# Five tap buffers instead of four, two gated tiles instead of three, and the decay sums one to a weight block

## The chip, the cores and the metric

The kernel runs on one core of one Trainium2 chip. The metric is the device time of one execution in microseconds (us), from the first instruction to the last with what lies around them. Five engines work at once, each through its own queue of instructions in order: PE (TensorE, matmuls; PEld is its weight load), DVE (VectorE), ACT (ScalarE), POOL (GpSimd) and SP (which issues DMAs).

## The reference, cut to what matters

One encoder block over 16 + 1024 tokens of width 1024. The part that the change touches is the start of the mixer: one wide projection, and then a depthwise convolution of 31 taps over the gated values (the conformer branch), a depthwise convolution of 7 taps (the state-space branch), and decays of a chunked state-space scan in both directions.

```python
u = h @ w_in
g_val, g_gate, z, xs, bs, cs, dtf, dtb, gate_conv, gate_ssm = jnp.split(u, offs, axis=-1)
a = g_val * jax.nn.sigmoid(g_gate)
a = dwconv(a, conv_dw_w, conv_dw_b)                      # 31 taps
a = jax.nn.silu(layernorm(a, conv_ln_g, conv_ln_b))
y_conv = a @ conv_out_w
xbc = jax.nn.silu(dwconv(jnp.concatenate([xs, bs, cs], axis=-1), ssm_conv_w, ssm_conv_b))   # 7 taps
...
a_cum = jnp.cumsum(adt, axis=-1)                         # per chunk of 128 tokens
decay_states = jnp.exp(a_cum[..., -1:] - a_cum)
y_off = jnp.einsum('bclgn,bcgepn,bcgel->bclgep', cc, states_in, jnp.exp(a_cum))
```

## The kernel before, in words

The program has four stretches: normalisation and the first projections; the rest of the input projection with the two convolutions; the scan over chunks; the output projections and the feed-forward part. The change lies in the second, which the list `AP` walks through in 26 weight blocks of 256 columns: g0 v0 z2 g1 x0 v1 z3 g2 bc0 v2 z4 g3 x1 v3 z5 bc1 x2 z6 x3 x4 bc2 x5 bc3 x6 x7 z7. Every product is three matmuls, since weights and operands are split in a high part (`wh`) and a remainder (`wl`).

**Weights.** `load_w` brings a block in two halves. For each half SP issues a DMA into a `wraw` buffer, ACT rounds it to `wh` (L138) and POOL subtracts to get the remainder `wl` (L139). `next_w` is called at the start of a block and loads one block ahead, so the weights of g2 are prepared around z3 and those of g3 around z4. A matmul of a block's first result tile goes through the eight slices of its weights in order, three matmuls for each; the first that needs the second half's remainder is the fifteenth.

**Gates and values.** A g block (`conf_gate`) writes sigmoids. A v block (`conf_val`) multiplies them with its own product into a gated tile `ap` (L501, DVE, out of PSUM, with high priority), for two tiles of 128 channels, and calls `conformer` for each. There 25 of the 31 taps are a chain on DVE (`conv`, L475 and L478). The other six are products of their own in `tap` tiles. In this text they are A, B, C, D (ACT, L513), E and F (POOL, L515), and A' to F' for the second tile of a block. POOL adds them up in place (L517): "add B" is B += A and frees A's buffer, "add C" is C += B and frees B's, and so on to "add F"; DVE adds F to its chain at the end (L481, `cacc`). The `tap` buffers are a ring of four.

**z blocks.** `z_block` makes eight result tiles of 24 matmuls (L272) in a ring of four PSUM buffers (`mm`). ACT empties each through a Silu (L275, into `w`). So the fifth tile can't begin until ACT has emptied the first. z2, z3, z4 and z5 follow v0, v1, v2 and v3 at once, and on ACT their evictions stand in the same queue as the tap products.

**Decays.** `decays` makes six sums over the chunks with two matmuls each (L423) into a PSUM tile `tp`, of which there is one buffer, and ACT writes the exponential of each (L424). They are `ea` (two), `wd` (two) and `dec` (two); DVE then multiplies `wd` by `dt` (L434). `decays` is a generator and goes on at each `yield`, once after each weight block from x0 on.

The order on each engine is made by a scheduler that moves instructions within their dependences; what it made of both programs is shown under the change.

Of the kernel before, what the change touches and what calls it, by code (L numbers as in the profile page):

```python
# [8 lines left out]
F32 = mybir.dt.float32  # L9
# [6 lines left out]
P = 128  # L16
D = 1024
KC = D // P
T = 1024
NM = 16  # L20
TT = T + NM
# [36 lines left out]
def tile_hybrid_block(  # L58
# [40 lines left out]
    m_le = const.tile([P, P], F32R, name="m_le")  # L99
    m_ge = const.tile([P, P], F32R, name="m_ge")  # L100
    ones_r = const.tile([P, P], F32R, name="ones_r")
    GP.memset(ones_r.bitcast(F32), 1.0)
    u_gt = const.tile([P, P], F32R, name="u_gt")
    u_lt = const.tile([P, P], F32R, name="u_lt")
# [125 lines left out]
    def ps_tp():  # L230
        return ps_now[0].tile([P, 512], F32, name="tp", tag="tp", bufs=ps_now[1]["tp"])

    def prm(r, i):
        return pr[:, r + i:r + i + 1]
# [50 lines left out]
    ea = sc.tile([P, NCH, 2 * NH], F32, name="ea")  # L285
    wd = sc.tile([P, NCH, 2 * NH], F32, name="wd")
    dec = sc.tile([P, NCH, 2 * NH], F32, name="dec")
    F_, B_ = slice(0, NH), slice(NH, 2 * NH)
# [130 lines left out]
    def decays():  # L419
        def sums(dst, dsl, m):  # L420
            ps = ps_tp()
            for i, a_ in enumerate((adh, adl)):
                PE.matmul(ps[:, :NCH * NH], lhsT=m, rhs=a_[:, :, dsl], start=(i == 0), stop=(i == 1))  # L423
            S.activation(out=dst[:, :, dsl], in_=ps[:, :NCH * NH].rearrange("p (c h) -> p c h", h=NH), func=AF.Exp)  # L424

        sums(ea, F_, m_le)
        sums(ea, B_, m_ge)
        yield
        sums(wd, F_, u_gt)
        sums(wd, B_, u_lt)  # L430
        yield
        sums(dec, F_, ones_r)
        sums(dec, B_, ones_r)
        V.tensor_tensor(out=wd, in0=wd, in1=dt, op=ALU.mult)  # L434
        yield
# [8 lines left out]
    cv = cv_ctx.enter_context(tc.tile_pool(name="cv", bufs=2))  # L444
    csum = cv.tile([P, T], F32, name="csum", bufs=1)

    xps = [cv.tile([P, TT + 6], F32, name=f"xp{i}", bufs=1) for i in range(4)]
    aps = [cv.tile([P, TT + 15], F32, name=f"ap{i}", bufs=1) for i in range(3)]
    for t in xps:
        GP.memset(t[:, :3], 0.0)  # L450
        GP.memset(t[:, TT + 3:], 0.0)
# [6 lines left out]
    def after(n, fn):  # L458

        later.append([n, fn])  # L460
# [7 lines left out]
    def conv(out_, src, w, taps, n, bias, add=None):  # L468

        acc = psB.tile([P, 1536], F32, name="acc", tag="acc", bufs=1)[:, :n]  # L470
        sl = lambda k: src[:, taps[k]:taps[k] + n]
        if bias is None:
            V.tensor_scalar(out=acc, in0=sl(0), scalar1=w(0), scalar2=None, op0=ALU.mult)
        else:
            V.tensor_scalar(out=acc, in0=sl(0), scalar1=w(0), scalar2=bias, op0=ALU.mult, op1=ALU.add)  # L475
        for k in range(1, len(taps)):
            last = k == len(taps) - 1 and add is None
            V.scalar_tensor_tensor(out=out_ if last else acc, in0=sl(k), scalar=w(k), in1=acc,  # L478
                                   op0=ALU.mult, op1=ALU.add)
        if add is not None:  # L480
            V.tensor_tensor(out=out_, in0=acc, in1=add, op=ALU.add)  # L481
# [12 lines left out]
    def conf_val(b):  # L494
        w = next_w(f"v{b}")
        for j in range(2):
            sg = sgs.pop(0)
            ap = next(rings["ap"])
            for t0, n, ps in proj(*w, j, CH3):
                with tc.high_priority():  # L500
                    V.tensor_tensor(out=ap[:, t0:t0 + n], in0=ps[:, :n], in1=sg[:, t0:t0 + n], op=ALU.mult)  # L501
            conformer(2 * b + j, ap)
            tick()

    def conformer(i, ap):

        w = lambda k: pr[:, R_CW + k * 8 + i:R_CW + k * 8 + i + 1]
        part = None
        for k in range(KCONF - NPC, KCONF):
            src = ap[:, 1 + k:1 + k + T]  # L510
            t = cv.tile([P, T], F32, name="tap", bufs=4)
            if k < KCONF - 2:
                S.activation(out=t, in_=src, func=AF.Copy, scale=w(k))  # L513
            else:
                GP.tensor_scalar(out=t, in0=src, scalar1=w(k), scalar2=None, op0=ALU.mult)  # L515
            if part is not None:
                GP.tensor_tensor(out=t, in0=t, in1=part, op=ALU.add)  # L517
            part = t
        acc = cv.tile([P, T], F32, name="cacc", bufs=2)
        conv(acc, ap, w, list(range(1, 1 + KCONF - NPC)), T, prm(R_CB, i), add=part)  # L520

        def done():
            SP.dma_start(out=d_a[i], in_=acc)
            if i == 0:
                GP.tensor_copy(out=csum, in_=acc)
            else:
                GP.tensor_tensor(out=csum, in0=csum, in1=acc, op=ALU.add)
            if i == KC - 1:
                SP.dma_start(out=d_cs, in_=csum)

        after(6, done)
# [45 lines left out]

    steps = {"g": conf_gate, "v": conf_val, "bc": bc_block, "x": xs_block, "z": z_in_turn}
    dc = decays()
    for n_, (k, i) in enumerate(AP):  # L580
        steps[k](i)
# [24 lines left out]
    def op_tile():  # L606
        h = opp_box[0].tile([P, 512], F32R, name="oph", tag="oph")
        l = opp_box[0].tile([P, 512], F32R, name="opl", tag="opl")
        return h, l
# [273 lines left out]
    for f in range(NCK + 1):  # L883
# [3 lines left out]
        if f % NTT == 0:  # L887
# [5 lines left out]
            t=lambda: nxt and nxt.select(4), T=lambda: nxt and nxt.scores(4),  # L893
# [102 lines left out]
    for hh in range(2):  # L996
        for i in range(KC):
            t = op_tile()
# [102 lines left out]
    sums, late = {}, []  # L1101
# [67 lines left out]
```

## Time and profile before

| | |
|---|---|
| median of 3 runs | 2341.51 us (2341.08 to 2342.58) |
| profiled execution | 2346.3 us, span 2344.1 us |
| PE busy | 2247.3 us, 96% of the span |
| DVE, ACT, POOL busy | 1445.8, 769.1 and 843.4 us (62%, 33%, 36%) |
| granted TensorE clock, mean | 0.983 of full speed |
| stretch of the 26 weight blocks | about 95 to 712 us |

PE is busy nearly all the time, so a change can gain at most what PE idles or runs at the lower clock. "Idle" of an instruction is the time that its engine did nothing just before it, with what ended that time. In the rows of stretches each engine has its busy time and, in brackets, its instructions; PEclk is the TensorE clock granted, as a share of full speed.

### The profile page before, as it was taken

The numbers are of one execution on the slowest core, as the hardware profiler recorded it, in microseconds if no ns is written. First come the engines' busy times: TensorE is split into PE (matmuls) and PEld (weight loads), VectorE is DVE, ScalarE is ACT, GpSimd is POOL, SyncE is SP. The second block draws the span as 40 slices with busy tenths as digits, with TensorE's granted clock in tenths as the row PEclk, the third lists the DMA queues.
The fourth block names the chain that finished last, engine by engine and source line by source line (L and its number), as shares of the span: only waits on it lengthen the run. The fifth ranks groups of instructions, "written<-read, shape, count | busy, mean of one in ns | idle before, by whom it ended". The sixth has DMA issues, their size and how long they took to land.

```text
span 2344.1 us, 31010 instructions
## 1 busy us (share of the span) xinstructions
PE 2247.3 (96%) x12103; PEld 1916.5 (82%) x12103; DVE 1445.8 (62%) x1726; ACT 769.1 (33%) x1385; POOL 843.4 (36%) x730
## 2 busy tenths in 40 slices
PE   8999899999999999888898999999999999999998
PEld 7999899999997666666666778898888888888887
DVE  4398898996771688888999675524233333333236
ACT  6333332323322445445544454214211111111112
POOL 3374654822112576777676241011101101101012
PEclk9999999999999999999999999999999999999999
DMA  4221222233236665656653652421111111111111
GB/s 137 87 72 64 73 76 69 82 104 104 89 102 200 186 198 155 201 155 194 210 167 120 227 177 90 146 66 37 43 47 54 37 54 54 36 54 54 36 54 72
DMA packets 223161, 245.29 MB, mean 105 GB/s; under 512 B 19112, under 2 KB 174360, under 8 KB 223016
## 3 DMA queue, kind: packets, MB, share of 16 engines
q1 hardware_dynamic: 210200, 221.89, 30.6%
q10 hardware_dynamic: 12816, 21.44, 2.5%
q8 instruction: 95, 1.56, 0.3%
q14 instruction: 50, 0.41, 0.1%
HBM read 174.23 MB, written 69.04 MB: 104 GB/s over the span
## 4 chain that ended last, share of the span: by engine, by line
PE 74%; DVE 7%; POOL 6%; issue 4%; DMA 3%; ACT 3%; SPq 0%; POOLq 0%; DVEq 0%; ACTq 0%
PE mm L196 31%; PE yo L196 12%; PE mm L272 6%; PE ss L196 5%; PE yd L196 4%; PE mm L1093 3%; PE yo L1093 3%; DVE gg L803 2%; POOL tap L517 2%; PE ss L1093 2%; PE yd L1093 2%; PE mm L1044 1%; PE yo L1044 1%; POOL wl L139 1%; PE tp L199 1%
## 5 line engine op out<-in xcount | busy, mean ns | idle before, releaser
L139 POOL TENSOR_TENSOR wl<-wraw,wh 128x1024 fp32r<-128x1024 f32 (+1 forms) x103 | 249.9, 2436 | 1116.5 <-ACT wh L138 1116.3
L196 PE MATMUL mm<-hnh,wh 128*128 128x352 f32 (+4 forms) x1248 | 428.0, 343 | 1.4 <-ACT w L275 0.9
L196 PE MATMUL mm<-hnl,wh 128*128 128x352 f32 (+4 forms) x1248 | 421.1, 337 | 0.4 <-DVE hnl L378 0.4
L196 PE MATMUL mm<-hnh,wl 128*128 128x352 f32 (+4 forms) x1248 | 418.7, 335 | 0.0
L138 ACT CAST wh<-wraw 128x1024 fp32r<-128x1024 f32 (+1 forms) x172 | 174.5, 1041 | 403.1 <-PE yd L1093 175.5
L139 DVE TENSOR_TENSOR wl<-wraw,wh 128x1024 fp32r<-128x1024 f32 x69 | 134.4, 1952 | 252.2 <-ACT wh L138 246.5
L478 DVE SCALAR_TENSOR_TENSOR acc<-ap,pr,acc 128x1024 f32<-128x1024 f32 x192 | 247.5, 1289 | 6.3
L196 PEld LDWEIGHTS mm<-hnh,wh 128*128 128x128 f32 x1248 | 235.7, 189 | 15.4 <-issue 2.4
L196 PEld LDWEIGHTS mm<-hnl,wh 128*128 128x128 f32 x1248 | 235.5, 189 | 12.4 <-issue 2.4
L196 PEld LDWEIGHTS mm<-hnh,wl 128*128 128x128 f32 x1248 | 235.4, 189 | 11.3
L196 PE MATMUL mm<-opl,wh 128*128 128x512 f32 x472 | 187.5, 397 | 8.0 <-DVE opl L625 7.9
L196 PE MATMUL mm<-oph,wh 128*128 128x512 f32 x472 | 190.0, 403 | 1.7 <-ACT oph L624 1.6
L803 DVE SCALAR_TENSOR_TENSOR gg<-cbb,dt,gg 128x128 f32<-128x128 f32 x256 | 167.4, 703 | 34.7 <-ACT gg L802 34.5
L196 PE MATMUL mm<-oph,wl 128*128 128x512 f32 x472 | 186.5, 395 | 0.0
L272 PE MATMUL mm<-wh,hnh 128*128 128x256 f32 x512 | 148.5, 291 | 12.2 <-ACT w L275 12.1
L478 DVE SCALAR_TENSOR_TENSOR acc<-xp,pr,acc 128x1040 f32<-128x1040 f32 x120 | 156.6, 1305 | 4.0
L272 PE MATMUL mm<-wl,hnh 128*128 128x256 f32 x512 | 147.6, 289 | 0.0
L272 PE MATMUL mm<-wh,hnl 128*128 128x256 f32 x512 | 147.4, 288 | 0.0
L196 PE MATMUL yo<-oph,wh 128*128 128x512 f32 x352 | 139.0, 395 | 0.0
L196 PE MATMUL yo<-opl,wh 128*128 128x512 f32 x352 | 138.9, 395 | 0.0
L196 PE MATMUL yo<-oph,wl 128*128 128x512 f32 x352 | 138.8, 394 | 0.0
L196 PEld LDWEIGHTS mm<-opl,wh 128*128 128x128 f32 x472 | 88.7, 188 | 32.2 <-DVE opl L625 10.7
(280 smaller groups left out, 4759.6 us busy)
## 6 DMA issues: line engine op xcount, KB each, us to landing
wraw<-in_w_in_dram SPq DMA_DIRECT2D x72, 512.0 KB, 3.7
xc<-d_x SPq DMA_DIRECT2D x64, 256.0 KB, 3.5
wraw<-in_w_gate_dram SPq DMA_DIRECT2D x22, 512.0 KB, 4.2
wraw<-in_w_up_dram SPq DMA_DIRECT2D x22, 512.0 KB, 4.1
wraw<-in_w_down_dram SPq DMA_DIRECT2D x22, 512.0 KB, 3.7
d_x<-xa ACTq DMA_DIRECT2D x16, 520.0 KB, 2.6
d_sz<-w ACTq DMA_DIRECT2D x64, 128.0 KB, 1.8
d_xt<-xt SPq DMA_DIRECT2D x32, 256.0 KB, 3.0
```

What stands on the lines that cost most here:

```text
L138: S.copy(out=h3[:, sl], in_=r3)
L139: (V if lo[i] == "v" else GP).tensor_tensor(out=l3[:, sl], in0=r3, in1=h3[:, sl].bitcast(F32), op=ALU.subtract)
L196: tie(PE.matmul(out_, **kw))
L199: tie(PE.transpose(out_, in_, ident_))
L272: PE.matmul(ps[:, :256], lhsT=a[:, sl], rhs=bb[:, k, :], start=(k == 0 and q_ == 0), stop=(k == KC - 1 and q_ == 2))
L478: V.scalar_tensor_tensor(out=out_ if last else acc, in0=sl(k), scalar=w(k), in1=acc, op0=ALU.mult, op1=ALU.add)
L517: GP.tensor_tensor(out=t, in0=t, in1=part, op=ALU.add)
L803: V.scalar_tensor_tensor(out=gg[0][:, h], in0=self.cbb, scalar=dt[:, self.c, self.hb:self.hb + HG][:, hs_], in1=gg[0][:, h], op0=ALU.mult, ...
L1044: PE.matmul(ps[:, :256], lhsT=a[:, sl], rhs=bb[:, k, :], start=(k == 0 and q_ == 0), stop=(k == KC - 1 and q_ == 2))
L1093: PE.matmul(ps, lhsT=a[:, sl], rhs=bb[:, k, t0:t0 + n], start=(k == 0 and q_ == 0), stop=(k == 1 and q_ == 2))
```

## The change

It edits three places: the loop over the six sums, which now yields after each of the first five instead of after each pair; the number of `ap` tiles, from three to two; the number of `tap` buffers, from four to five. Line numbers behind L430 are smaller by four in the changed program.

```diff
-        sums(ea, F_, m_le)
-        sums(ea, B_, m_ge)
-        yield
-        sums(wd, F_, u_gt)
-        sums(wd, B_, u_lt)
-        yield
-        sums(dec, F_, ones_r)
+        for dst, dsl, m in ((ea, F_, m_le), (ea, B_, m_ge), (wd, F_, u_gt), (wd, B_, u_lt), (dec, F_, ones_r)):
+            sums(dst, dsl, m)
+            yield
         sums(dec, B_, ones_r)
         V.tensor_tensor(out=wd, in0=wd, in1=dt, op=ALU.mult)
         yield
...
-    aps = [cv.tile([P, TT + 15], F32, name=f"ap{i}", bufs=1) for i in range(3)]
+    aps = [cv.tile([P, TT + 15], F32, name=f"ap{i}", bufs=1) for i in range(2)]
...
-            t = cv.tile([P, T], F32, name="tap", bufs=4)
+            t = cv.tile([P, T], F32, name="tap", bufs=5)
```

On ACT, before, the second tile of v1 and the start of z3 stand like this (`w` with a number is the tile that an eviction of z3 writes).

```order
L138 CAST wh<-wraw 128x1024
L513 ACTIVATE tap<-ap_1103,pr 128x1024 x3
L424 ACT_TABLE_LOAD
L424 ACTIVATE wd<-tp 128x9x32
L513 ACTIVATE tap<-ap_1103,pr 128x1024
L424 ACTIVATE wd<-tp 128x9x32
L138 CAST wh<-wraw 128x1024
L275 ACT_TABLE_LOAD
L275 ACTIVATE w_2442<-mm 128x256
L275 ACTIVATE w_2470<-mm 128x256
```

On ACT, with the change, the same place:

```order
L138 CAST wh<-wraw 128x1024
L424 ACT_TABLE_LOAD
L424 ACTIVATE ea<-tp 128x9x32
L509 ACTIVATE tap<-ap_1104,pr 128x1024 x4
L138 CAST wh<-wraw 128x1024
L275 ACT_TABLE_LOAD
L275 ACTIVATE w_2432<-mm 128x256
L275 ACTIVATE w_2460<-mm 128x256
```

One exponential stands here instead of two, ahead of the taps; all four taps stand together; the second half of g2's weights is still rounded between the taps and the first eviction. At z4 the changed program has the same eight rows, with `dec` for `ea`, where before it had both casts, three taps, the first eviction, the fourth tap and the second eviction; at z2 and z5 there is no exponential, and the order is both casts, four taps, evictions, where before the fourth tap stood behind the first eviction.

On POOL, before, the taps of v2's two tiles:

```order
L517 TENSOR_TENSOR tap<-tap 128x1024
L515 TENSOR_SCALAR tap<-ap_1104,pr 128x1024
L517 TENSOR_TENSOR tap<-tap 128x1024 x2
L515 TENSOR_SCALAR tap<-ap_1104,pr 128x1024
L517 TENSOR_TENSOR tap<-tap 128x1024 x2
L139 TENSOR_TENSOR wl<-wraw,wh 128x1024 x2
L517 TENSOR_TENSOR tap<-tap 128x1024 x2
```

On POOL, with the change, the same taps:

```order
L513 TENSOR_TENSOR tap<-tap 128x1024
L511 TENSOR_SCALAR tap<-ap_1103,pr 128x1024
L513 TENSOR_TENSOR tap<-tap 128x1024
L511 TENSOR_SCALAR tap<-ap_1103,pr 128x1024
L513 TENSOR_TENSOR tap<-tap 128x1024 x3
L139 TENSOR_TENSOR wl<-wraw,wh 128x1024
L513 TENSOR_TENSOR tap<-tap 128x1024
L511 TENSOR_SCALAR tap<-ap_1104,pr 128x1024
L513 TENSOR_TENSOR tap<-tap 128x1024 x2
L511 TENSOR_SCALAR tap<-ap_1104,pr 128x1024
L513 TENSOR_TENSOR tap<-tap 128x1024
L139 TENSOR_TENSOR wl<-wraw,wh 128x1024
```

F comes one add earlier, which leaves the first tile's seven instructions seven. The two remainders of g3's weights, which stood together ahead of the second tile's adds, are parted: the second now stands behind add B', E', add C', add D', F' and add E'. The remainders of g2's weights were parted before the change too and stay so; those at z2 and z5 stay together.

On PE, the end of v1 and the start of z3 (`tp` is the one buffer of the sums):

```order
 L196 MATMUL mm<-hnl_150,wh 128x336
 L196 MATMUL mm<-hnh_142,wl 128x336
-L423 MATMUL tp<-adh,u_gt 128x288
-L423 MATMUL tp<-adl,u_gt 128x288
+L423 MATMUL tp<-adh,m_ge 128x288
+L423 MATMUL tp<-adl,m_ge 128x288
 L272 MATMUL mm<-wh,hnh_135 128x256
 L272 MATMUL mm<-wl,hnh_135 128x256
```

The second sum of `ea` takes the place of the first of `wd`. The second of `wd`, which stood before the last matmul of z3's second tile, is gone from there: it comes at the end of g2. The sums now stand at the ends of x0, v1, z3, g2, bc0 and v2. DVE's product of `wd` and `dt` moves from the chain of v1's first tile into that of its second, behind 16 of the 24 L478 taps. SP's queue is unchanged, and from z5 on the other queues differ in a few places of ACT alone, where a Silu and a copy change places.

## Rows read from the trace of the kernel before

**Rows 1.** Waits of PE, 95 to 700 us: total, times, longest.

```profile
PE mm L272 <- ACT w L275: 12.1, 5, 3.9
```

**Rows 2.** Timeline of PE: start, duration, instruction, idle before it and releaser.

```profile
145.16 0.39 PE L272 MATMUL mm<-wh,hnh 128*128 128x256 f32 x1 [1.05 <-ACT w L275]
150.77 0.38 PE L272 MATMUL mm<-wh,hnh 128*128 128x256 f32 x1 [2.50 <-ACT w L275]
...
243.02 0.61 PE L423 MATMUL tp<-adh,u_lt 128*128 128x288 f32 x1 [6.74 <-ACT wd L424]
...
343.56 0.38 PE L272 MATMUL mm<-wh,hnh 128*128 128x256 f32 x1 [0.74 <-ACT w L275]
350.55 0.58 PE L272 MATMUL mm<-wh,hnh 128*128 128x256 f32 x1 [3.89 <-ACT w L275]
...
448.87 0.58 PE L272 MATMUL mm<-wh,hnh 128*128 128x256 f32 x1 [3.92 <-ACT w L275]
...
950.85 1.10 PE L196 MATMUL yo<-xw,bt 128*128 128x512 f32 x2 [2.16 <-DVE y L837]
```

**Rows 3.** Stretches: length, busy PE, PEld, DVE, ACT, POOL, then PEclk, DMA share, GB/s.

```profile
150.70:156.00 5.30, 5.23 (x31) 5.23 (x32) 5.16 (x5) 1.55 (x5) 5.20 (x3) 0.68 0.31 102
243.00:247.00 4.00, 3.98 (x19) 3.98 (x20) 0.81 (x1) 2.29 (x3) 3.92 (x2) 0.52 0.47 131
350.50:356.50 6.00, 5.95 (x29) 5.95 (x30) 5.80 (x5) 1.54 (x5) 5.90 (x3) 0.53 0.28 92
448.80:456.80 8.00, 7.93 (x43) 7.93 (x44) 7.74 (x7) 1.55 (x5) 7.82 (x4) 0.61 0.25 85
...
950.00:953.00 3.00, 2.15 (x10) 1.53 (x11) 3.00 (x6) 0.84 (x2) 1.57 (x2) 1.00 0.76 238
```

**Rows 4.** Timeline of ACT: the second tile of v2 and z4.

```profile
331.38 2.00 ACT L138 CAST wh<-wraw 128x1024 fp32r<-128x1024 f32 x2 [5.22 <-issue]
...
342.08 1.15 ACT L513 ACTIVATE tap<-ap,pr 128x1024 f32<-128x1024 f32 x1 [1.33 <-POOL tap L517]
343.14 0.36 ACT L275 ACTIVATE w<-mm 128x256 f32<-128x256 f32 x1
349.08 1.15 ACT L513 ACTIVATE tap<-ap,pr 128x1024 f32<-128x1024 f32 x1 [5.58 <-POOL tap L517]
...
350.14 0.36 ACT L275 ACTIVATE w<-mm 128x256 f32<-128x256 f32 x1
```

**Rows 5.** Timeline of POOL: the end of v1's first tile, and v2's taps.

```profile
240.01 2.35 POOL L139 TENSOR_TENSOR wl<-wraw,wh 128x1024 fp32r<-128x1024 f32 x1
...
326.67 2.85 POOL L515 TENSOR_SCALAR tap<-ap,pr 128x1024 f32<-128x1024 f32 x1
...
342.00 4.74 POOL L139 TENSOR_TENSOR wl<-wraw,wh 128x1024 fp32r<-128x1024 f32 x2
346.70 4.79 POOL L517 TENSOR_TENSOR tap<-tap 128x1024 f32<-128x1024 f32 x2
```

**Rows 6.** Timeline of ACT at v1's second tile: table load and exponential.

```profile
241.26 1.28 ACT L424 ACT_TABLE_LOAD   x1
242.55 0.41 ACT L424 ACTIVATE wd<-tp 128x288 f32<-128x288 f32 x1
```

**Rows 7.** Chain that ended last: z6's eight tiles, undisturbed.

```profile
506.15 22.72 PE mm L272 x192
```

**Rows 8.** Timeline of PE: a matmul near the start of g2 and of g3.

```profile
262.50 0.32 PE L196 MATMUL mm<-hnh,wh 128*128 128x352 f32 x1
...
361.64 0.33 PE L196 MATMUL mm<-hnh,wh 128*128 128x352 f32 x1
```

**Rows 9.** Timeline of DVE: three rows of v1 and v2.

```profile
246.19 1.57 DVE L434 TENSOR_TENSOR wd<-wd,dt 128x576 f32<-128x576 f32 x1 [8.70 <-ACT wd L424]
...
299.45 1.23 DVE L481 TENSOR_TENSOR cacc<-acc,tap 128x1024 f32<-128x1024 f32 x1
...
323.91 0.53 DVE L501 TENSOR_TENSOR ap<-mm,sg 128x352 f32<-128x352 f32 x1
```

## Prediction

> **What bounds the kernel now.** I read the waits of PE first, then its timeline at each wait, then the granted clock behind it, then ACT and POOL there. In the stretch of the weight blocks PE idles in six places and nowhere else [rows 1, 2]: 1.05 and 2.50 us in z2, 6.74 in z3, 0.74 and 3.89 in z4, 3.92 in z5, together 18.84. Five of them wait for ACT to empty a PSUM buffer of a z block; that is the 12.1 of [rows 1]. The 6.74 is a sum of the decays that waits for the one `tp` buffer.
>
> Four of the six cost more than their length, since the clock falls from its upper level (2.4 GHz) to the lower (1.2) behind them [rows 3]. Loss = length x (1 - PEclk): 5.3 x 0.32 = 1.7 us behind the 2.50, 4 x 0.48 = 1.9 behind the 6.74, 6 x 0.47 = 2.8 behind the 3.89, 8 x 0.39 = 3.1 behind the 3.92. So the places cost 1.05 + 2.50 + 1.7 = 5.2 (z2), 8.6 (z3), 7.4 (z4) and 7.0 (z5), together 28.3 us. That is the most the change can give.
>
> Why they exist is seen best at z4 [rows 4, 5]. C' starts at 342.08, when POOL is through with add F (its next row begins at 342.00). ACT then empties z4's first tile and meets D', which must wait until 349.08. POOL has meanwhile made two weight remainders (342.00, 4.74 us) and the first of two adds from 346.70: add B' ends at 349.1 and frees the buffer that D' takes. ACT empties the second tile at 350.14 and PE goes on at 350.55. Four buffers are one too few: A to D fill the ring, E and F take A's and B's, A' to C' take C's, D's and E's, and D' has to wait for A'.
>
> **The change part by part.** *Five tap buffers.* F now takes A's, and A' to D' take B's, C's, D's and E's; E's is freed by add F. So D' starts where C' started, 7.0 us earlier (349.08 - 342.08). POOL's first-tile work is the same seven instructions in another order and ends at the same time.
>
> z2: no exponential stands here. C' ended ahead of the table load of the first eviction, and D' now does, at the same time, so the 1.05 stays; the 2.50 and its 1.7 go. Gain 4.2.
>
> z5: D' takes the place of C' and the first eviction follows it by no more than before, when it made PE wait nowhere. The 3.92 and its 3.1 go. Gain 7.0.
>
> z3 and z4 differ. Ahead of the first eviction ACT now has D', a cast and a table load: in z3 240.1 (POOL is through with add F at 240.01 [rows 5]) + 1.15 + 1.0 [rows 4] + 1.28 [rows 6] + 0.4 = 243.95. z3 starts 6.74 and two tiles ahead of 243.02, at 230.6; a tile takes 22.72 / 8 = 2.84 [rows 7], so four are done at 241.95: PE idles 2.05 for the first eviction. In z4 the same sum from 342.08 gives 345.9. The changed order puts v2's first taps ahead of a Silu that cost about 0.9 us, so I take 345.0. Four tiles are done at 342.82 (343.56 - 0.74) + 0.25 for the sum that now stands ahead of z4 = 343.1; PE idles 1.9, or 2.8 without the 0.9.
>
> Next, what is late behind it. g2 and g3 need the second half of their remainders at their fifteenth matmul, 14 x 0.163 = 2.3 us after their start. Before, that was 262.50 + 2.3 = 264.8 and 361.64 + 2.3 = 363.9 [rows 8]. POOL now makes it, in both blocks, eighth from the end of add F: two remainders of 2.37, four adds of 2.40 and two products of 2.85 [rows 5] (add B', E', add C', add D', F', add E' between the remainders) = 20.1 us, so at 260.2 and at 342.0 - 0.9 + 20.1 = 361.2. PE would be there at 244.0 + 11.4 + 0.3 (a sum) + 2.3 = 258.0, and at 345.05 + 11.4 + 2.3 = 358.7, so it waits 2.2 and 2.5 us in the middle of a tile. The gains are set by the remainders: z3 264.8 - 260.2 = 4.6, with 0.25 for the sum that left the start of g2 4.8; z4 363.9 - 361.2 = 2.7 (bound: 1.8 without the 0.9).
>
> What these waits do to the clock is the open price. Idle times of 1.05, 0.74 and of 2.16 at 950.85 were not followed by the lower level (1.00 in 950 to 953), those from 2.50 on were [rows 2, 3]. The first waits (2.05 and 1.9) are nearest to 2.16: no fall. If it falls there all the same, the loss only shortens the second wait. The second ones (2.2 and 2.5) lie at the edge: 0 to 2.8 us each. I take one fall, 1.7, the loss behind the 2.50.
>
> *The sums.* They are twelve matmuls before and after. The 6.74 of z3 goes as the sum that waited is now at the end of g2, with a whole block for the exponential ahead of it. ACT has one table load more in all (1.28, [rows 6]); two of the loads lie on the path, those ahead of the evictions of z3 and z4, and are in the sums above. The next ACTIVATE starts 1.29 after the load [rows 6]. The Trainium skill, ScalarE: Activation LUTs, What ACT_TABLE_LOAD costs, speaks against the edit: a switch of set costs 1.28 us and as much again of drain, 2.66 in all, and functions should be grouped by set. By 2.66 PE would idle about 3.4 us in z3 and in z4 and surely lose clock, but the remainders come when they come; an estimate from that page is 17 us of gain in all. The row shows the 1.28 without the drain.
>
> DVE no longer waits 8.70 us for `wd` in v1's first tile [rows 9]. It meets that product in the second tile, before the exponential at the end of g2 is there: by the same rows about 5 us of wait. It then enters v2 some 1.5 us later than before relative to PE, which its waits for PE there take up; the gated tiles come up to 1 us later, with a PSUM tile to spare.
>
> *Two gated tiles.* The second tile of v2 is first written at 323.91, and now goes into the buffer of v1's second tile, whose chain ends by 299.45 [rows 9]: 24 us to spare, less the 1.5. The other pairs have more. The edit costs nothing as long as DVE is not 24 us late; without that cover PE would stand still for the difference, four PSUM tiles later.
>
> Sum: 4.2 + 4.8 + 2.7 + 7.0 = 18.7, less 1.7 = 17.0 us. From z5 on the queues are as before, and from 460 us on PE has no idle time in this stretch, so the rest moves as a whole. Against the profiled execution 2346.3 - 17.0 = 2329.3; this execution lies 4.8 above the median of the runs, so 2324.5 for the median.
>
> **The rivals.**
> *Weights late.* The remainders cost more than worked out: POOL's taps start as before (no 0.9), both second waits lose clock, 2.8 each. Then z3 and z4 give 6.6 - 5.6 = 1, with z2 and z5 12: 2329. For it: POOL's queue is without gaps there. Against: the falls may just as well come early, where they cost nothing.
> *More than that.* ACT and POOL reach v2's and v1's taps earlier than I have them, and no clock is lost: z3 and z4 give up to 10 instead of 7.5, in all 21: 2320.5.
> *Nothing changes.* PE's waits go but DVE, not PE, is the true bound there (7.74 busy of 8.00 in [rows 3]), and the stretch ends when its chains end. Gain 0 to 4: about 2340. Against: DVE stood still for 8.70 at once and PE did not follow it there.
> *Slower.* With two gated tiles a v block's eviction waits for a chain two tiles back. If DVE runs later than 24 us against PE in v2 and v3, each further us stops PE in both blocks; from about 9 us more per block (2 x 9 > 17) the change is slower, e.g. 2346 at 11. Nothing in the trace puts DVE that late, as it waits for PE's products ahead of each v block.
>
> **How the numbers follow.** As forecast, with no, one or two falls of the clock (2322.8 to 2326.2): 0.55. Weights late (to 2333): 0.25. More: 0.1. Nothing changes: 0.06. Slower: 0.04. The range 2320 to 2333 holds the first three. A measurement tells about 0.2%, 4.7 us, from no change; the first three are beyond it: faster 0.9, same 0.06, slower 0.04.
>
> **What would show it.** Right: no idle time of PE in z5, one of about 1 us in z2; no wait at a sum of the decays; in z3 and z4 one idle time of about 2 us for the first eviction; a wait for POOL's `wl` in the first tile of g2 and g3; D' starting as add F ends. Wrong: D' still behind add B', idle time at L501 of a v block for a gated tile, or DVE's `wd` product stopping PE.

## The result, and the profile after

The changed kernel takes 2325.56 us (median of 6 runs, 2323.84 to 2330.77); beside it the kernel before took 2342.61 (6 runs, 2341.08 to 2343.57). The ratio is 0.9932, with a 95% interval of 0.9920 to 0.9945: 17.05 us faster. The forecast was 2324.5 and 17.0 us.

| | before | after |
|---|---|---|
| profiled execution, span | 2346.3, 2344.1 us | 2329.2, 2327.1 us |
| PE busy | 2247.3 us | 2240.5 us |
| granted TensorE clock, mean | 0.983 | 0.988 |

The two largest waits of PE from 95 to 700 us (line waited at, releaser: total, times, longest), which answer [rows 1]:

```profile
PE mm L272 <- ACT w L275: 5.0, 3, 2.7
PE mm L196 <- POOL wl L139: 4.3, 2, 2.3
```

The wait of a sum (L423) is gone, and a wait for POOL's remainders is new. The same from PE's timeline (start, duration, instruction, idle before it and releaser), all five idle times over 0.5 us of this stretch, which answer [rows 2]:

```profile
144.42 0.39 PE L272 MATMUL mm<-wh,hnh 128*128 128x256 f32 x1 [0.92 <-ACT w L275]
239.22 0.39 PE L272 MATMUL mm<-wh,hnh 128*128 128x256 f32 x1 [2.68 <-ACT w L275]
255.38 0.60 PE L196 MATMUL mm<-hnh,wl 128*128 128x352 f32 x1 [2.03 <-POOL wl L139]
337.12 0.39 PE L272 MATMUL mm<-wh,hnh 128*128 128x256 f32 x1 [1.43 <-ACT w L275]
353.28 0.43 PE L196 MATMUL mm<-hnh,wl 128*128 128x352 f32 x1 [2.27 <-POOL wl L139]
```

So z2 keeps 0.92, z3 has 2.68 and then 2.03 in g2, z4 has 1.43 and then 2.27 in g3, and z5 has none: 9.33 us instead of 18.84. The granted clock in the stretches around them (columns as in [rows 3]):

```profile
150.00:156.00 6.00, 6.00 (x53) 6.00 (x52) 5.76 (x6) 0.77 (x2) 5.92 (x3) 1.00 0.29 100
239.20:243.20 4.00, 3.98 (x33) 3.98 (x34) 3.90 (x4) 1.36 (x4) 3.90 (x3) 1.00 0.67 222
255.30:261.30 6.00, 5.92 (x27) 5.92 (x28) 5.83 (x6) 2.06 (x2) 6.00 (x4) 0.72 0.36 94
353.20:359.20 6.00, 5.92 (x27) 5.92 (x28) 5.86 (x5) 2.31 (x2) 5.91 (x4) 0.72 0.34 91
440.00:448.00 8.00, 8.00 (x61) 8.00 (x60) 7.74 (x7) 2.65 (x4) 7.92 (x4) 1.00 0.16 53
```

It is at its upper level (2.4 GHz) in z2, behind the 2.68 of z3, and in z5. It falls behind the 2.03 and the 2.27: 6 x 0.28 = 1.7 us each.

ACT's timeline, which answers [rows 4]: D' of v1's second tile with what follows it, then D' of v2's and of v3's.

```profile
235.39 1.15 ACT L509 ACTIVATE tap<-ap,pr 128x1024 f32<-128x1024 f32 x1 [1.33 <-POOL tap L513]
236.45 1.02 ACT L138 CAST wh<-wraw 128x1024 fp32r<-128x1024 f32 x1
237.49 1.28 ACT L275 ACT_TABLE_LOAD   x1
238.79 0.66 ACT L275 ACTIVATE w<-mm 128x256 f32<-128x256 f32 x2
...
333.28 1.15 ACT L509 ACTIVATE tap<-ap,pr 128x1024 f32<-128x1024 f32 x1 [1.33 <-POOL tap L513]
...
431.22 1.15 ACT L509 ACTIVATE tap<-ap,pr 128x1024 f32<-128x1024 f32 x1 [1.32 <-POOL tap L513]
```

POOL's remainders in the same places, which answer [rows 5]: the one right behind add F in each block, and the one that g2 and g3 wait for.

```profile
235.31 2.39 POOL L139 TENSOR_TENSOR wl<-wraw,wh 128x1024 fp32r<-128x1024 f32 x1
...
252.97 2.35 POOL L139 TENSOR_TENSOR wl<-wraw,wh 128x1024 fp32r<-128x1024 f32 x1
...
333.21 2.40 POOL L139 TENSOR_TENSOR wl<-wraw,wh 128x1024 fp32r<-128x1024 f32 x1
...
350.87 2.36 POOL L139 TENSOR_TENSOR wl<-wraw,wh 128x1024 fp32r<-128x1024 f32 x1
...
431.15 4.76 POOL L139 TENSOR_TENSOR wl<-wraw,wh 128x1024 fp32r<-128x1024 f32 x2
```

In all three blocks D' starts as POOL goes on from add F (235.39 and 235.31, 333.28 and 333.21, 431.22 and 431.15): the buffer it waits for is E's. In z3 a rounding and a table load still stand between D' and the first eviction at 238.79, and PE goes on at 239.22. The remainders for g2 and g3 end at 255.32 and 353.23, and PE goes on at 255.38 and 353.28.

DVE, which answers [rows 9]: the product of `wd`, the last row of v1's second chain, and the first write into its buffer.

```profile
280.84 0.99 DVE L430 TENSOR_TENSOR wd<-wd,dt 128x576 f32<-128x576 f32 x1 [7.77 <-ACT wd L424]
...
292.40 1.23 DVE L477 TENSOR_TENSOR cacc<-acc,tap 128x1024 f32<-128x1024 f32 x1
...
316.99 0.52 DVE L497 TENSOR_TENSOR ap<-mm,sg 128x352 f32<-128x352 f32 x1
```

The chain is through at 293.63 and its buffer is written at 316.99: 23.4 us to spare with two gated tiles.

### The profile page after: what moved, and what is told of

It is laid out like the page before. It is cut to its first block, busy times and chain, and to the rows that moved or that the text cites. A ratio compares the mean times of both kernels' runs of the same rounds, so it can differ in the third digit from the quotient of the medians.

```text
span 2327.1 us, 31009 instructions
## 1 busy us (share of the span) xinstructions
PE 2240.5 (96%) x12103; PEld 1909.8 (82%) x12103; DVE 1440.0 (62%) x1726; ACT 769.5 (33%) x1386; POOL 839.0 (36%) x729
## 4 chain that ended last, share of the span: by engine, by line
PE 75%; DVE 7%; POOL 6%; issue 4%; DMA 4%; ACT 3%; SPq 0%; POOLq 0%; ACTq 0%; DVEq 0%
PE mm L196 33%; PE yo L196 12%; PE mm L272 5%; PE ss L196 5%; PE yd L196 4%; PE mm L1089 3%; PE yo L1089 3%; DVE gg L799 2%; POOL tap L513 2%; PE ss L1089 2%; PE yd L1089 2%; PE mm L1040 1%; PE yo L1040 1%; ACT gg L798 1%; PE tp L199 1%
```

## The experiments

For all of them, one table of PE's timeline: the time from the first matmul of one block to the first of the next, each a difference of two starts. "g1 to z4" covers g1, x0, v1, z3, g2, bc0 and v2, "z4 to z5" covers z4, g3, x1 and v3; so each of the two holds the same sums in all kernels that end them before z4. The last column runs from z2's start to the first matmul behind z7.

| kernel | median, us | z2 | g1 to z4 | z4 to z5 | z5 | bc1, x2 | z2 to the end |
|---|---|---|---|---|---|---|---|
| before | 2342.6 | 28.33 | 170.37 | 98.94 | 30.02 | 45.74 | 579.42 |
| after | 2325.6 | 23.90 | 168.28 | 97.05 | 22.95 | 45.74 | 563.95 |
| after, second profile | 2325.9 | 23.92 | 166.75 | 95.49 | 22.95 | 45.74 | 560.88 |
| five buffers, sums in pairs | 2326.2 | 23.91 | 170.80 | 92.16 | 22.96 | 45.74 | 561.60 |
| sums spread, four buffers | 2344.0 | 28.18 | 170.54 | 98.53 | 29.84 | 45.75 | 578.86 |
| two gated tiles alone | 2342.3 | 26.80 | 170.53 | 99.05 | 28.56 | 45.75 | 576.71 |
| remainders of g2, g3 ahead | 2322.0 | 23.92 | 166.00 | 93.01 | 22.95 | 45.75 | 557.66 |
| no sum at v1 and v2 | 2322.7 | 23.91 | 161.81 | 92.21 | 23.87 | 51.12 | 558.94 |
| both, sums from g1 on | 2318.4 | 23.90 | 162.25 | 91.51 | 22.94 | 45.75 | 552.37 |
| both, sums from x0 on | 2318.0 | 23.92 | 161.82 | 92.23 | 23.89 | 45.75 | 553.63 |

**The buffers without the spread.** The kernel before with these two lines changed:

```diff
-    aps = [cv.tile([P, TT + 15], F32, name=f"ap{i}", bufs=1) for i in range(3)]
+    aps = [cv.tile([P, TT + 15], F32, name=f"ap{i}", bufs=1) for i in range(2)]
-            t = cv.tile([P, T], F32, name="tap", bufs=4)
+            t = cv.tile([P, T], F32, name="tap", bufs=5)
```

> Five tap buffers and two gated tiles, with the sums of the decays in pairs as before. Theory (the buffers bring the gain, and the spread of the sums gives with one hand and takes with the other): z2 and z5 gain as with the whole change (4.4 and 7.1 us); in z3 the sum still waits its 6.74 us, since the exponential it waits for still stands behind a tap that starts as add F ends, so 0; in z4, where no exponential stands now, both remainders are made together, the 3.89 and the 2.8 behind it go and about 0.7 stays: 6.7. In all 18.2 below 2342.6: 2324.4 us, no wait for a remainder in g2 or g3. Rival (the spread sums bring what z3 and z4 gained, the buffers z2 and z5 alone): 11.5 below, 2331 us. Rival (two gated tiles cost something of their own that the spread hides): above 2331, with idle time at L501 or a PE wait for a gated product.

Measured: 2326.24 us (5 runs), ratio 0.9932 (0.9919 to 0.9944), the same as the whole change. All idle times of PE over 0.5 us in the stretch:

```profile
145.91 0.39 PE L272 MATMUL mm<-wh,hnh 128*128 128x256 f32 x1 [0.94 <-ACT w L275]
239.32 0.61 PE L423 MATMUL tp<-adh,u_lt 128*128 128x288 f32 x1 [5.55 <-ACT wd L424]
262.66 0.40 PE L423 MATMUL tp<-adh,ones_r 128*128 128x288 f32 x1 [0.77 <-ACT dec L424]
340.28 0.39 PE L272 MATMUL mm<-wh,hnh 128*128 128x256 f32 x1 [0.60 <-ACT w L275]
```

As the theory had it: the sum in z3 still waits (5.55 instead of 6.74), z4 keeps 0.60 and gains 6.8, no remainder is late, and no product of a v block is held up. From z2 to the end this profile lies 579.42 - 561.60 = 17.8 us below that of before, where 18.2 were expected; 0.77 goes to a second sum, which now waits in g2. The median came out 1.8 us above the 2324.4 expected, and the profile doesn't show where the rest of that lies.

**The spread without the buffers.** The loop over the six sums alone, with three gated tiles and four buffers.

> The spread of the sums alone, with four tap buffers and three gated tiles. Theory: z2 and z5 stay as they were before. In z3 and z4 every eviction now stands behind the fourth tap D', which still waits for add B', and behind a table load: the 6.74 of z3 becomes an idle time of about 5.6 for the first eviction (about nothing gained, with the clock behind it), and in z4 the 0.74 and 3.89 become one of about 8 to 9 us. In all 0 to 5 us slower than before: 2345 us (2342 to 2348). Rival (the spread is worth the 6.74 and the 1.9 behind it by itself): 2334 us. Rival (it does nothing alone): 2342.6.

Measured: 2343.99 us (11 runs), ratio 1.0005 (0.9996 to 1.0014): nothing. PE's idle times over 0.5 us:

```profile
145.16 0.39 PE L272 MATMUL mm<-wh,hnh 128*128 128x256 f32 x1 [1.05 <-ACT w L275]
150.76 0.58 PE L272 MATMUL mm<-wh,hnh 128*128 128x256 f32 x1 [2.50 <-ACT w L275]
247.93 0.58 PE L272 MATMUL mm<-wh,hnh 128*128 128x256 f32 x1 [6.50 <-ACT w L275]
348.13 0.58 PE L272 MATMUL mm<-wh,hnh 128*128 128x256 f32 x1 [5.29 <-ACT w L275]
448.48 0.58 PE L272 MATMUL mm<-wh,hnh 128*128 128x256 f32 x1 [3.93 <-ACT w L275]
```

The 6.74 of the sum became 6.50 for the first eviction, behind the same tap. In z4 8 to 9 us were expected and 5.29 came: the spread parts the two remainders there, so that POOL makes one of them, not both, ahead of the add that D' waits for, and add F ends 340.48 - 331.31 = 9.2 us behind the start of z4 instead of 342.00 - 331.29 = 10.7. POOL's first remainder there, the adds of B' and C', and D' on ACT:

```profile
340.48 2.41 POOL L139 TENSOR_TENSOR wl<-wraw,wh 128x1024 fp32r<-128x1024 f32 x1
342.86 4.77 POOL L513 TENSOR_TENSOR tap<-tap 128x1024 f32<-128x1024 f32 x2
...
345.23 1.15 ACT L509 ACTIVATE tap<-ap,pr 128x1024 f32<-128x1024 f32 x1 [2.58 <-POOL tap L513]
```

The wait for the sum had been the place where D' became visible, not its cause.

**Two gated tiles alone.** The kernel before with `range(2)` for the `ap` tiles.

> The kernel before with two gated tiles instead of three, nothing else. Theory (the second buffer comes free 24 us before it is written): no change, 2342.5 us, PE's six idle times as before. Rival (two gated tiles hold up PE's products of v2 and v3, which the change's gain hid): 2345 or more, with a wait of PE for DVE at a v block.

Measured: 2342.26 us (11 runs), ratio 1.0000 (0.9992 to 1.0009). The six idle times come again (1.06, 2.48, 6.68, 0.74, 3.90, 3.91), and PE waits for no gated product. The edit is free. By the code a gated tile (1055 columns) is a little larger than a tap buffer (1024, of the same type), so two and five take no more memory than three and four; five tap buffers beside three gated tiles were not run.

**The late remainders.** In the changed kernel, the second remainder of g2 and that of g3 made ahead of F' and add E' on POOL, where the trace has add E' ahead of F' then:

```diff
-    def load_w(view, lo):
+    def load_w(view, lo, first=False):
...
-            (V if lo[i] == "v" else GP).tensor_tensor(out=l3[:, sl], in0=r3, in1=h3[:, sl].bitcast(F32), op=ALU.subtract)
+            with (tc.high_priority() if first else ExitStack()): (V if lo[i] == "v" else GP).tensor_tensor(out=l3[:, sl], in0=r3, in1=h3[:, sl].bitcast(F32), op=ALU.subtract)
...
-            ready.append((k, load_w(view, lo)))
+            ready.append((k, load_w(view, lo, k in ("g2", "g3"))))
```

> The changed kernel with the remainder of the second half of g2's and of g3's weights moved two places ahead on POOL (before F' and add E' of the second tile, 5.25 us sooner); nothing else moves on any engine. Theory (these two remainders set the second waits, 2.03 and 2.27, and the lower clock behind each, 1.7 and 1.7): they go, and 7.7 us with them: 2317.9 us. Rival (the waits are set by the rounding of the weights or by their transfer, the remainder only comes last): the waits stay, 2325.6. Rival (F' and add E', now 2.4 us later, stop DVE and through it PE): the waits go, another comes in v2 or v3's products, 2322 or more.

Measured: 2321.96 us (4 runs), ratio to before 0.9911 (0.9898 to 0.9925); 3.6 below the changed kernel, not 7.7. Both waits for `wl` are gone, and nothing takes their place; these are all idle times over 0.5 us behind z2, and the clock behind the first of them:

```profile
240.38 0.38 PE L272 MATMUL mm<-wh,hnh 128*128 128x256 f32 x1 [2.69 <-ACT w L275]
336.00 0.39 PE L272 MATMUL mm<-wh,hnh 128*128 128x256 f32 x1 [1.44 <-ACT w L275]
```

```profile
240.30:244.30 4.00, 3.92 (x20) 3.92 (x21) 3.90 (x4) 1.07 (x4) 3.90 (x3) 0.57 0.66 219
```

So the remainders did set the second waits. What is lacking of the 7.7 goes with the clock, as far as the profiles show: here it fell behind the 2.69 in z3, where it had stayed up in the profile of the changed kernel, and z3 took 27.48 us instead of 25.93. From z2 to the end this profile lies 563.95 - 557.66 = 6.3 us below that of the changed kernel with its two falls, and 560.88 - 557.66 = 3.2 below the second one of that kernel, which follows.

**The changed kernel again.**

> The changed kernel once more, for a second profile: moving the late remainders ahead took 3.6 us off the median, where the two waits and the lower clock behind them are 7.7 in the changed kernel's profile, whose execution (2329.2 us) is 3.7 above its median. Theory (the idle times are the same in every execution, the falls of the clock behind idle times of 2.0 to 2.7 us are not): the five idle times come again within 0.1 us, 0.92, 2.68, 2.03, 1.43 and 2.27, but the lower clock stands behind others of them or behind fewer. Rival (an idle time of a given place loses the same clock each time): the lower clock stands behind the 2.03 and the 2.27 again, and behind no other.

Measured: 2325.90 us (5 runs); its profiled execution took 2325.0 us. The idle times are the same five; this is the clock behind 2.69, 2.01 and 2.30:

```profile
239.00:243.00 4.00, 4.00 (x36) 4.00 (x36) 3.90 (x4) 1.16 (x3) 3.90 (x3) 1.00 0.69 232
255.00:259.00 4.00, 4.00 (x25) 4.00 (x26) 3.89 (x4) 0.27 (x1) 4.00 (x2) 1.00 0.48 133
351.30:355.30 4.00, 3.98 (x25) 3.98 (x26) 3.90 (x4) 0.11 (x1) 4.00 (x2) 1.00 0.47 131
```

No fall is granted in these rows, nor in any stretch of 5 us from 95 to 700, which are all at 1.00: the idle times belong to the kernel, the falls behind those of 2.0 to 2.7 us to the execution. The two profiles of one kernel differ by 563.95 - 560.88 = 3.1 us in this stretch, all of it in g2 and g3.

**No sum at the ends of v1 and v2.** In the changed kernel:

```diff
-        if n_ > DCN:
+        if n_ > DCN and (k, i) not in (("v", 1), ("v", 2)):
             next(dc, None)
```

> The changed kernel with no sum at the ends of v1 and v2 (they stand at the ends of x0, z3, g2, bc0, z4 and g3), so that no exponential and no table load stand ahead of the first eviction of z3 and z4. Both remainders of g2 and of g3 then stand together behind add F, but those of bc1, behind z5, are parted. Theory (the exponentials ahead of the evictions cost what is left in z3 and z4): in z3 2.68 becomes about 0.5, the 2.03 and the 1.7 behind it go: 5.9; in z4 1.43, 2.27 and 1.7 go: 5.4; in z5 a first wait of about 1.2 comes, and a wait of bc1 for its parted remainder of about 3.8 with about 2 of clock: -7. In all 4.3 below 2325.6: 2321.3 us. Rival (the exponentials cost nothing, the waits are POOL's alone): first waits of z3 and z4 stay near 2.7 and 1.4; about 2327. Rival (the parted remainder of bc1 costs nothing): 2314.

Measured: 2322.66 us (4 runs), ratio to before 0.9918 (0.9904 to 0.9931); 2.9 below the changed kernel, where 4.3 was expected. PE's idle times over 0.5 us behind z2:

```profile
236.67 0.38 PE L272 MATMUL mm<-wh,hnh 128*128 128x256 f32 x1 [0.60 <-ACT w L275]
422.15 0.39 PE L272 MATMUL mm<-wh,hnh 128*128 128x256 f32 x1 [0.91 <-ACT w L275]
439.69 0.66 PE L196 MATMUL mm<-hnh,wl 128*128 128x352 f32 x1 [3.68 <-POOL wl L139]
```

Place by place the idle times are near what was expected (0.5, 1.2 and 3.8): what the changed kernel kept in z3 and z4, the waits for the remainders among it, came from the sums at the ends of v1 and v2. That the gain is 2.9 and not 4.3 goes with the clock: the 4.3 counted both falls of the changed kernel's first profile, and from z2 to the end this kernel lies 563.95 - 558.94 = 5.0 us below that profile, but 560.88 - 558.94 = 1.9 below the second. With an exponential ahead of the taps, the order that the scheduler makes has the second rounding behind the taps, and the remainder that needs it behind POOL's adds. The same order has now befallen bc1, though no exponential stands beside v3's second taps (D', the second rounding right behind it, and the remainder that bc1 waits for):

```profile
419.73 1.15 ACT L509 ACTIVATE tap<-ap,pr 128x1024 f32<-128x1024 f32 x1 [1.33 <-POOL tap L513]
420.79 1.03 ACT L138 CAST wh<-wraw 128x1024 fp32r<-128x1024 f32 x1
...
437.30 2.34 POOL L139 TENSOR_TENSOR wl<-wraw,wh 128x1024 fp32r<-128x1024 f32 x1
```

So an exponential beside the taps is not the only thing that brings this order about; what does so here was not tested. It costs bc1 3.68 and the clock: bc1 and x2 take 51.12 instead of 45.74.

**Both.** The last two kernels together, with the remainders of g1 and bc1 ahead too. One begins its sums at x0; the other, with `DCN = 2`, at g1, so that they are through one block earlier.

> The changed kernel with the sums at the ends of x0, z3, g2, bc0, z4 and g3, and POOL's remainders of g1, g2, g3 and bc1 ahead of the taps that wait beside them. It differs from the kernel without sums at v1 and v2 in one place, bc1's second remainder, which is 5.25 us sooner. Theory: the idle times of that kernel stay (0.93 in z2, 0.60 in z3, 0.91 in z5), its 3.68 in bc1 goes with the 1.7 of lower clock behind it: 5.4 below its 2322.7, 2317.3 us. Rival (bc1 waits for something else too, or the second tile's F' and add E', now later, stop DVE): 2320 or more.

> The changed kernel with the sums at the ends of g1, x0, z3, g2, bc0 and z4 (none ahead of the evictions of z3 and z4), and POOL's remainders of g1, g2, g3 and bc1 ahead of the taps that wait beside them. Theory: z2 keeps 0.93; z3 has one idle time of about 1.3 (the rounding of g2's second half stands ahead of the first eviction), z4 about 0.3, no wait in g2, g3 and bc1. Of the 9.3 us of idle time of the changed kernel's profile 2.5 are left, and no lower clock behind them: 6.8 to 10.2 below the changed kernel, 2317 us (2315 to 2319). Rival (the sum at the end of g1 holds up PE or ACT there): an idle time in x0, about 2319.

Measured: 2317.98 us for sums from x0 on, ratio to before 0.9894 (0.9881 to 0.9907), and 2318.36 for sums from g1 on, 0.9893 (0.9881 to 0.9906), 4 runs each. The first keeps three idle times and the second two; these are the first's:

```profile
144.67 0.38 PE L272 MATMUL mm<-wh,hnh 128*128 128x256 f32 x1 [0.94 <-ACT w L275]
237.10 0.38 PE L272 MATMUL mm<-wh,hnh 128*128 128x256 f32 x1 [0.59 <-ACT w L275]
422.63 0.39 PE L272 MATMUL mm<-wh,hnh 128*128 128x256 f32 x1 [0.93 <-ACT w L275]
```

bc1 and x2 are back at 45.75, 5.37 below the kernel without sums at v1 and v2 (5.4 expected). In the second z3 idles 0.63 where about 1.3 was expected. Both versions are about 7.4 us faster than the changed kernel and the fastest found.

## Why the prediction was right

*Where PE idles and what one more buffer does.* Right. Idle times were forecast as about 1 in z2, 2.05 in z3, 2.2 in g2, 1.9 in z4, 2.5 in g3 and none in z5; they are 0.92, 2.68, 2.03, 1.43, 2.27 and none. z2 gained 28.33 - 23.90 = 4.4 (4.2 forecast) and z5 30.02 - 22.95 = 7.1 (7.0).

*z3 and z4.* The sum of the two was nearly right, 7.1 us where 7.5 were forecast, but its parts were off by 1.2 and 0.7 in opposite directions; that they cancel is luck. Take the second profile, where the clock stayed up: g1 to z4 gained 170.37 - 166.75 = 3.6 where 4.8 was forecast, and z4 to z5 98.94 - 95.49 = 3.4 where 2.7 was. The working chain was right (POOL's remainder eighth behind add F: 20.1 us forecast; 255.32 - 235.31 = 20.0 and 353.23 - 333.21 = 20.0 measured). What was off is where add F ends. In v1 the prediction left it where it was, but it ends 10.3 us behind the start of z3 (235.31 - 225.02) instead of 9.5 (240.01 - 230.55); in v2 it is earlier, as taken, by 10.7 - 9.05 = 1.7 rather than 0.9. Another 0.3 is what the stretch from g2 to z4 takes above its idle time (71.70 with, 69.39 without the wait: 2.31 for 2.01), and g3 has 0.2 of the same kind. The later add F of v1 comes with the spread of the sums: with five buffers and the sums in pairs it ends 236.31 - 226.97 = 9.3 us behind the start of z3. It does not come from the exponential that then stands ahead of A': without the sum at v1 it ends 235.12 - 224.54 = 10.6 us behind. The remainders that start at its end, in these two kernels:

```profile
236.31 2.35 POOL L139 TENSOR_TENSOR wl<-wraw,wh 128x1024 fp32r<-128x1024 f32 x1
...
235.12 4.77 POOL L139 TENSOR_TENSOR wl<-wraw,wh 128x1024 fp32r<-128x1024 f32 x2
```

*The clock.* This term, one fall of 1.7 us, is the least sure one, and the runs show why. In the first profile there were two falls, in the second none, for the same idle times within 0.03. From z2's start to the end the first is 579.42 - 563.95 = 15.5 us below the profile of before and the second 579.42 - 560.88 = 18.5; the forecast of 17.0 lies in the middle, and so does the difference of the medians. The spans differ by more, 2344.1 - 2327.1 = 17.0 and 2344.1 - 2322.9 = 21.2; 1.5 and 2.7 of that lie outside these blocks, where the prediction had nothing. The falls of before are no more certain: with two gated tiles alone, whose idle times are those of before within 0.1, z2 took 26.80 us instead of 28.33 and z5 28.56 instead of 30.02. So the clock's share in z2 and z5 is confirmed against one profile of before alone, and that the total came out within 0.1 us of the measured 17.05 is partly luck. The rule that was taken from [rows 2, 3] (none up to 2.16, a fall from 2.50 on) does not hold: 2.68 was followed by none and 2.03 by one.

*The sums.* The step was right that two table loads come to lie on the path, and right that they would not cost a drain as well. The eviction in z3 starts 1.30 us behind the load's start (237.49 to 238.79), and z3 idled 2.68; what this is above the forecast 2.05 goes with add F, 0.8 later. The Trainium skill, ScalarE: Activation LUTs, What ACT_TABLE_LOAD costs, gives 2.66 for a switch with its drain, which by an estimate from that page would have made it 3.4; the trace does not agree. What the prediction missed is how little the edit is worth: it credited the end of the 6.74 to the spread, while the spread alone changed nothing (1.0005) and the buffers alone gave all of it (0.9932). With five buffers the spread takes the sum's 5.55 out of z3 and puts two first waits and two late remainders in its place; the order with pairs takes 561.60 us from z2 to the end, the spread 563.95 and 560.88, and the medians are the same. Taken elsewhere, the same six sums are worth 3 us more, and 7.4 with the remainders ahead.

*DVE and the gated tiles.* `wd` makes DVE wait 7.77 in v1's second tile, where about 5 was forecast; PE did not follow, as said. The gated tile had 23.4 us to spare, where 24 less 1.5 was forecast. The rival "slower" is out: the two gated tiles alone measured 1.0000, and PE waits for no gated tile. "Nothing changes" is out by the gain itself.

*The other rivals.* "Weights late" needed both second waits to lose clock; the first profile is such an execution, at 2329.2. "More" needed no loss and an earlier POOL; the second profile has no loss, but z3 and z4 gave 7.1 and not 10.

## What to carry to other kernels

When a ring of buffers between two engines is one short, the wait shows up wherever the blocked queue is needed next: on a PSUM buffer, or on a sum that only waits for its exponential; find the instruction at the head of the blocked queue before crediting an edit that moves the symptom. An operation that is put ahead of a burst on ACT can delay everything whose order follows from ACT's, here the rounding and then POOL's remainder, and the wait shows a whole block later; look for the place where nothing is due behind it. Where several edits come as one change, run each alone: here one carried all of it, one was free, and one gave nothing until its sums were moved to other places, with the buffers there.

## What the runs showed of the hardware

The lower clock behind an idle time of PE is not set by the length of the idle time alone. In the stretch of the weight blocks, in the ten profiles here, idle times of 0.59 to 1.45 us were never followed by the lower level, and those of 3.68 to 6.74 always (0.50 granted over the 4 us behind 5.55 and 6.50, 0.58 behind 3.68). Between them it went both ways in the same place: behind 2.68 and 2.69 in z3 the clock stayed at 1.00 in both profiles of the changed kernel, and fell to 0.57 behind 2.69 in the kernel with the remainders ahead; behind 2.03 and 2.27 in g2 and g3 it fell to 0.57 and 0.66 over the next 4 us in the first profile, and behind 2.01 and 2.30 in the second profile of the same kernel it stayed at 1.00; behind 2.50 and 2.48 in z2 it was 0.68 before and 1.00 with two gated tiles:

```profile
149.60:155.60 6.00, 5.98 (x50) 5.99 (x51) 5.76 (x6) 1.54 (x4) 5.90 (x3) 1.00 0.29 98
```

The same view behind the 3.68 that bc1 waits in the kernel without sums at v1 and v2:

```profile
439.60:443.60 4.00, 3.91 (x15) 3.91 (x16) 3.89 (x4) 0.09 (x1) 4.00 (x3) 0.58 0.46 131
```

What decides between the two was not settled. It is 3.1 us between the two profiles of the changed kernel in this stretch. The executions of that kernel spread over 7 us (2323.8 to 2330.8); how much of that is the clock was not shown. The last two kernels, whose idle times are all under 1 us, lose nothing to it in this stretch.
